# Low parts of 48 mix weight tiles per layer: a negating ScalarE copy and an accumulating DMA in place of subtractions

## The chip, the cores and the metric

The kernel runs on one core of a Trainium2 chip. The metric is the device time of one execution in microseconds (us), as the median of several runs. One execution was also taken by the hardware profiler. Engines are named as the profile names them: PE (TensorE matmul), PEld (its weight load), DVE (VectorE), ACT (ScalarE), POOL (GpSimd) and SP (SyncE, which only issues DMAs here).

## What is computed

A decoder trunk of two layers over 512 tokens of width 1024. Each layer has a token mixer with three gated branches, then a convolutional feed-forward part, each followed by a LayerNorm on a residual sum:

```python
h = layer_norm(x, ln_in_g, ln_in_b)
for l in range(DEPTH):                       # 2
    z = h @ w_in + b_in                      # pooling, conformer, q/k/v, indexer, three gates
    y_pool = pool_mixer(u_pool) @ w_pool_out
    y_conv = conformer_conv(u_conv) @ w_conv_out   # 31 taps, LayerNorm, swish
    y_attn = dsa_attention(...) @ w_attn_out       # indexer keeps the top 128 keys of a query
    merged = g0 * y_pool + g1 * y_conv + g2 * y_attn
    h = layer_norm(ALPHA * h + merged @ w_o)
    u = causal_dwconv(h @ w_up)
    h = layer_norm(ALPHA * h + (silu(gate) * val) @ w_down)
```

All of it is float32. A product of two float32 matrices is made of three passes: each operand is split into a high part (its value rounded to the matmul type `float32r`) and a low part (value minus high part), and high x high, high x low and low x high are summed.

## The kernel before, in words

**Weight tiles.** The weights of a layer are packed into 123 tiles of 128 x 1024 float32 (512 KB), in the order of use. `Weights.emit` (L66) prepares one: SP loads `w_raw` from memory (L70, two buffers), ACT copies it to the high part `w_hi` (L74, which rounds), and one engine subtracts, `w_lo = w_raw - w_hi` (L78). That engine is DVE (one instruction of 1024 columns), or POOL for the tiles listed in `W.side` (two instructions of 512 columns). In the mixer these are the nine tiles of `MIX_SIDE`; some more are listed around the end of each output projection. `w_hi` and `w_lo` have four buffers each. `Weights.take` (L83) hands out the next tile and first prepares all up to two tiles ahead.

**The mixer's tiles of a layer.** Tiles 0 to 2 are used beside the LayerNorm before. 3 to 16 are the other projections (indexer, pooling, conformer, v, q). 17 to 30 belong to branch A: a small tile that four steps share, four gate tiles, a second such five, four gates of branch C. 31 to 44 are the same for branch B. 45 to 48 are the attention output, 49 to 56 the output projection `w_o` in two halves of four. An ordinary projection tile makes 24 matmuls of 512 columns (`proj`, L282); its product lies in a PSUM bank of the kind "a", of which there are three, until ACT or DVE has read it.

**Work beside the tiles.** Generators are pumped between tiles (`step`, L398): on DVE the indexer (weighted sum of heads into `mask`, L475 and L477, then 16 rounds of MAX8 and MATCH_REPLACE, L484 and L485, for each of three query blocks), on ACT and POOL the conformer taps (ACT scales a shifted copy into `cvt`, L589; POOL adds it to `cv`, L590), then the softmax attention. In branch A DVE multiplies gate and branch product into `part` (L729), which frees a bank.

**The end of the mixer.** For each of eight column blocks `jt` DVE multiplies the last gate with the attention product (L762), POOL adds it to `part` (L763), ACT makes the high part of half the sum (L765) and DVE the low part (L766). After `jt == 3` the residual's LayerNorm scale and shift is issued: 16 POOL instructions (`residual`, L215, L220 and L221). Tiles 49 to 52, the first half of the output projection, each multiply two of the eight merged blocks (L316 to L318).

**Order.** Every engine executes its own instructions in order and waits in front of the first whose inputs or buffers aren't ready. The order is set before the run by a scheduler that places instructions by priority; the weight preparation runs at high priority (L73), so it moves up as far as its buffers let it.

Of the kernel before, what the change touches and what calls it, by code (L numbers as in the profile page):

```python
# [11 lines left out]
AF = mybir.ActivationFunctionType  # L12
ALU = mybir.AluOpType
# [30 lines left out]
N_CHUNK = 123  # L44
NSPLIT = {"mix": 3, "ffn": 3}
LAG = 2
MIX_SIDE = range(24, 42, 2)
ISSUE_ORDER = mybir.DependencyInfo(mybir.DependencyClass.NoSync, mybir.DependencyReason.DATA)
SIDE = 4
LN_POOL = ()  # L50
# [4 lines left out]
class Weights:  # L55
    def __init__(self, tc, w, raw_pool, split_pool, look, nchunk):
        self.tc, self.nc, self.w = tc, tc.nc, w
        self.raw_pool, self.split_pool = raw_pool, split_pool
        self.look = look
        self.n = nchunk  # L60
        self.emitted = 0
        self.used = 0
        self.ready = []
        self.side = set()

    def emit(self, upto):  # L66
        nc = self.nc
        while self.emitted < min(upto, self.n):
            raw = self.raw_pool.tile([P, D], F32, name="w_raw", tag="w_raw")
            nc.sync.dma_start(out=raw, in_=self.w[self.emitted])  # L70
            hi = self.split_pool.tile([P, D], F32R, name="w_hi", tag="w_hi")
            lo = self.split_pool.tile([P, D], F32R, name="w_lo", tag="w_lo")
            with self.tc.high_priority():  # L73
                nc.scalar.activation(hi, raw, AF.Copy)  # L74
                eng = nc.gpsimd if self.emitted in self.side else nc.vector
                for c in range(2 if self.emitted in self.side else 1):
                    cs = slice(512 * c, 512 * c + 512) if self.emitted in self.side else slice(0, D)
                    eng.tensor_tensor(out=lo[:, cs], in0=raw[:, cs], in1=hi[:, cs].bitcast(F32),  # L78
                                      op=ALU.subtract)
            self.ready.append((hi, lo))  # L80
            self.emitted += 1

    def take(self, look=None):  # L83
        self.emit(self.used + 1 + (self.look if look is None else look))
        self.used += 1
        return self.ready.pop(0)

# [2 lines left out]
def trunk_kernel(ctx, tc, x, positions, w, poolw, params, lnv, cons, out):  # L90
    nc = tc.nc
# [9 lines left out]
    W = Weights(tc, w, raw_pool, split_pool, 2, DEPTH * N_CHUNK)  # L101
# [253 lines left out]
    def mix(l, head, prev, ln, nxt):  # L355
        es = ExitStack()
        with es:
# [5 lines left out]
            def q_slot(tag, dt=F32R):  # L363
                return slot(tag, {"qa": 6, "qb": 4, "qc": 4}[tag], dt)
# [7 lines left out]
            def p_slot(dt=F32):  # L372
                return slot("part", 9, dt, [P, 528])
# [8 lines left out]
                return half_par[:, l, ct:ct + 1]  # L382

            bga, bgb = [], []
            W.side.update(l * N_CHUNK + i for i in MIX_SIDE)

            def pump(q, n):
                while q and n > 0:
# [366 lines left out]
            for jt in range(KT):  # L755
# [8 lines left out]
                hi, lo = q_slot("qa" if jt < 6 else "qb"), p_slot(F32R)[:, 0:L]  # L764
# [47 lines left out]
    for l in range(DEPTH):  # L812
        ffn_head = new_head("ffn")
        norm = mix(l, mix_head, norm, (1 + 2 * l, False), ffn_head)
        last = l == DEPTH - 1
        mix_head = None if last else new_head("mix")
        norm = ffn(l, ffn_head, norm, (2 + 2 * l, last), mix_head)
# [99 lines left out]
```

## Time and profile before

| | us |
|---|---|
| median of 3 runs | 1548.92 (1548.11 to 1550.29) |
| the profiled execution, its own time | 1548.56 |
| its span in the profile | 1546.8 |
| PE busy | 1467.5 (95%) |
| DVE busy | 1007.5 (65%) |
| ACT busy | 683.6 (44%) |
| POOL busy | 538.1 (35%) |

The span runs from the first to the last instruction. A busy share is a mean over stages that are limited by different things, so a share says little by itself. Matmuls overlap: one of 512 columns lasts 0.39 us, but the next starts before it ends, so PE can be shown busy all the time and still execute at different rates; the count of matmuls in a stretch tells more.

### The profile page before, as it was taken

The page shows a single profiled execution, that of the slowest core. Times are in us where ns is not written, and L with a number is a line of the kernel's source. Part 1 is how long each engine was busy: PE and PEld are TensorE (multiplying, and loading weights), DVE is VectorE, ACT ScalarE, POOL GpSimd, SP SyncE. Part 2 cuts the span into 40 slices and gives each one's busy share as a digit, 9 for nine tenths or more (in the row PEclk, how much of TensorE's full clock was granted, in tenths as well). Part 3 has the DMA queues.
Part 4 walks back from the last instruction along what each step waited for, and adds up shares of the span by engine and source line. Part 5 has one row for each costly group of instructions (what it writes and reads, how often), then busy time and mean ns, then how long its engine had stood idle before and what let it go on. Part 6 is the DMA issues. An engine that isn't in the chain of part 4 may idle for free.

```text
span 1546.8 us, 18617 instructions
## 1 busy us (share of the span) xinstructions
PE 1467.5 (95%) x6850; PEld 1218.1 (79%) x6850; DVE 1007.5 (65%) x1600; ACT 683.6 (44%) x1064; POOL 538.1 (35%) x395
## 2 busy tenths in 40 slices
PE   5998789999999999999999978999999999999997
PEld 5876678887888888888898756888878788888886
DVE  6799998756665555523268999976556655554234
ACT  5666636542444444421256664555326444443110
POOL 2357842209471111100134687231375511111004
PEclk9999999999999999999999989999999999999999
DMA  4422222223233333333234222222333333332331
GB/s 147 143 85 83 68 82 69 69 86 105 72 123 106 96 95 96 98 98 101 86 106 122 74 63 82 83 69 72 105 94 105 119 106 96 96 96 87 105 100 64
DMA packets 45019, 145.02 MB, mean 94 GB/s; under 512 B 6144, under 2 KB 7808, under 8 KB 44928
## 3 DMA queue, kind: packets, MB, share of 16 engines
q1 hardware_dynamic: 37632, 133.55, 28.1%
q10 hardware_dynamic: 7296, 10.29, 2.3%
q8 instruction: 54, 0.88, 0.2%
q14 instruction: 37, 0.30, 0.1%
HBM read 137.00 MB, written 2.10 MB: 90 GB/s over the span
## 4 chain that ended last, share of the span: by engine, by line
PE 70%; DVE 15%; POOL 7%; issue 4%; ACT 2%; DMA 2%; ACTq 0%; POOLq 0%; DVEq 0%
PE pb_a L289 15%; PE pb_a L290 15%; PE pb_a L291 15%; POOL h L221 3%; DVE w_lo L78 2%; POOL h L220 2%; PE pb_a L318 2%; PE pb_a L317 2%; PE pb_a L316 2%; DVE mask L477 2%; DVE mask L485 2%; PE pb_p L318 2%; PE pb_p L317 2%; PE pb_p L316 2%; PE pb_s L318 1%
## 5 line engine op out<-in xcount | busy, mean ns | idle before, releaser
L289 PE MATMUL pb_a<-hT_hi,w_hi 128*128 128x512 f32 (+1 forms) x1264 | 498.4, 394 | 35.8 <-DVE part L729 26.6
L78 DVE TENSOR_TENSOR w_lo<-w_raw,w_hi 128x1024 fp32r<-128x1024 f32 x210 | 290.3, 1383 | 339.9 <-ACT w_hi L74 338.9
L290 PE MATMUL pb_a<-hT_lo,w_hi 128*128 128x512 f32 (+1 forms) x1264 | 496.9, 393 | 0.0
L291 PE MATMUL pb_a<-hT_hi,w_lo 128*128 128x512 f32 (+1 forms) x1264 | 496.3, 393 | 0.0
L74 ACT ACTIVATE w_hi<-w_raw 128x1024 fp32r<-128x1024 f32 x246 | 260.6, 1059 | 400.0 <-PE pb_a L290 166.3
L289 PEld LDWEIGHTS pb_a<-hT_hi,w_hi 128*128 128x128 f32 x1264 | 241.2, 191 | 87.6 <-DVE part L729 29.9
L291 PEld LDWEIGHTS pb_a<-hT_hi,w_lo 128*128 128x128 f32 x1264 | 241.1, 191 | 47.4
L290 PEld LDWEIGHTS pb_a<-hT_lo,w_hi 128*128 128x128 f32 x1264 | 241.0, 191 | 46.5
L78 POOL TENSOR_TENSOR w_lo<-w_raw,w_hi 128x512 fp32r<-128x512 f32 x72 | 103.7, 1462 | 269.9 <-ACT w_hi L74 269.9
L800 POOL TENSOR_TENSOR fu<-fu 128x512 f32<-128x512 f32 x44 | 61.2, 1391 | 356.5 <-DVE fu L794 356.5
L590 POOL TENSOR_TENSOR cv<-cv,cvt 128x512 f32<-128x512 f32 x92 | 143.1, 1557 | 54.1 <-ACT cvt L589 46.5
L589 ACT ACTIVATE cvt<-cv,par 128x512 f32<-128x512 f32 x92 | 65.5, 721 | 28.0 <-POOL cv L590 27.7
L799 ACT ACTIVATE fu<-fu 128x512 f32<-128x512 f32 x44 | 27.8, 632 | 81.7 <-DVE fu L794 81.7
L794 DVE SCALAR_TENSOR_TENSOR fu<-pb_a,par,fu 128x510 f32<-128x510 f32 x82 | 61.4, 749 | 2.7
L791 ACT ACTIVATE fu<-pb_a,par 128x512 f32<-128x512 f32 x82 | 62.4, 761 | 0.0
L792 DVE SCALAR_TENSOR_TENSOR fu<-pb_a,par,fu 128x511 f32<-128x511 f32 x82 | 60.9, 743 | 0.0
L220 POOL TENSOR_TENSOR h<-h,gbt 128x512 f32<-128x512 f32 x32 | 52.1, 1660 | 18.3 <-DMA gbt<-in_lnv_dram 18.3
L683 ACT ACTIVATE qa<-qa,mx 128x128 f32<-128x128 f32 (+3 forms) x64 | 35.8, 560 | 51.1 <-DVE mx L680 48.2
L484 DVE MAX8 m<-mask 128x8 f32<-128x256 f32 (+2 forms) x96 | 52.8, 553 | 1.0
L208 ACT ACTIVATE gbt<-pb_a,par 128x128 f32<-128x128 f32 x96 | 35.7, 467 | 39.9 <-PE pb_a L200 39.9
L485 DVE MATCH_REPLACE8 mask<-m,mask 128x256 f32<-128x256 f32 (+2 forms) x96 | 51.9, 541 | 0.1
L316 PE MATMUL pb_a<-w_hi,g_hi 128*128 128x512 f32 x132 | 51.3, 389 | 0.0
(289 smaller groups left out, 2539.5 us busy)
## 6 DMA issues: line engine op xcount, KB each, us to landing
w_raw<-in_w_dram SPq DMA_DIRECT2D x246, 512.0 KB, 3.6
gbt<-in_lnv_dram ACTq DMA_DIRECT2D x20, 256.0 KB, 3.5
h<-in_x_dram SPq DMA_DIRECT2D x4, 512.0 KB, 5.5
t<-t ACTq DMA_DIRECT2D x32, 64.0 KB, 2.0
out_dram<-h SPq DMA_DIRECT2D x8, 256.0 KB, 2.0
part<-t ACTq DMA_DIRECT2D x32, 48.0 KB, 3.1
part<-t ACTq DMA_DIRECT2D x16, 64.0 KB, 4.1
par<-in_params_dram SPq DMA_DIRECT2D x2, 143.5 KB, 6.5
```

Source lines behind the costliest of these rows:

```text
L74: nc.scalar.activation(hi, raw, AF.Copy)
L78: eng.tensor_tensor(out=lo[:, cs], in0=raw[:, cs], in1=hi[:, cs].bitcast(F32), op=ALU.subtract)
L220: G.tensor_tensor(out=hb, in0=hb, in1=gb[0][c], op=ALU.mult)
L289: T.matmul(o, wh, xh(xc), start=(i == 0), stop=False)
L290: T.matmul(o, wh, xl(xc), start=False, stop=False)
L291: T.matmul(o, wl, xh(xc), start=False, stop=(i == n - 1))
L316: first = T.matmul(po[b], lh(k, b), wh, start=(k == 0), stop=False)
L318: T.matmul(po[b], ll(k, b), wh, start=False, stop=(k == nk - 1))
L485: V.match_replace(out=sc, in_to_replace=m8, in_values=sc, imm_value=FILL)
L589: A.activation(tm, hp[c][:, i:i + L], AF.Copy, scale=tap(i))
L590: G.tensor_tensor(out=pacc, in0=pacc, in1=tm, op=ALU.add)
L791: A.activation(t, o, AF.Identity, bias=par[:, l, PO_FB + ct:PO_FB + ct + 1], scale=tapw(2))
```

## The change

For tiles 7 to 54 of each layer (48 of 123), the low part is made in another way. ACT copies the raw tile into `w_lo` with scale -1, which gives minus the high part. POOL issues a DMA that reads the weight tile from memory once more and adds it to what lies in `w_lo`. ACT makes `w_hi` as before. DVE and POOL execute no subtraction for these tiles, and the list `MIX_SIDE` is gone; the other tiles are as before. When the tile that is taken is one of the 48, `take` prepares up to three tiles ahead, not two.

```diff
-MIX_SIDE = range(24, 42, 2)
+MIX_DMA = range(7, 55)
...
+            if self.emitted in self.by_dma:
+                with self.tc.high_priority():
+                    nc.scalar.activation(lo, raw, AF.Copy, scale=-1.0)
+                    nc.gpsimd.dma_start(out=lo, in_=self.w[self.emitted], accum_op=ALU.add)
+                    nc.scalar.activation(hi, raw, AF.Copy)
+                self.ready.append((hi, lo))
+                self.emitted += 1
+                continue
...
     def take(self, look=None):
-        self.emit(self.used + 1 + (self.look if look is None else look))
+        look = self.look + (self.used in self.by_dma) if look is None else look
+        self.emit(self.used + 1 + look)
...
-            W.side.update(l * N_CHUNK + i for i in MIX_SIDE)
+            W.by_dma.update(l * N_CHUNK + i for i in MIX_DMA)
```

The scheduler orders the whole program anew. Line numbers after the change are 10 higher behind `take`. Three places are shown.

ACT in branch A, first layer, before: a high part, then the gate's tanh out of the bank (`t<-pb_a`, L715), then indexer and tap work.

```order
L74 ACTIVATE w_hi_1584<-w_raw_1582 128x1024
L715 ACTIVATE t_1545<-pb_a_1520,half_par_89 128x512
L472 ACTIVATE u_1632<-pb_s_1629 128x512
L589 ACTIVATE cvt_1421<-cv_1021,par_74 128x512
L589 ACTIVATE cvt_1425<-cv_1021,par_74 128x512
```

The same gate after the change:

```order
L78 ACTIVATE w_hi_1537<-w_raw_1535 128x1024
L76 ACTIVATE w_lo_1538<-w_raw_1535 128x1024
L725 ACTIVATE t_1567<-pb_a_1542,half_par_89 128x512
L482 ACTIVATE u_1661<-pb_s_1658 128x512
L599 ACTIVATE cvt_1371<-cv_986,par_74 128x512
```

The negated copy stands between the high part and the reading of the bank. In both versions the tile that is prepared here is the third after the one whose product is read.

POOL in branch A, first layer, before, around the second of the tiles that it subtracts there, between conformer taps (`cv`):

```order
L590 TENSOR_TENSOR cv_1361<-cv_1361,cvt_1579 128x512
L78 TENSOR_TENSOR w_lo_1881<-w_raw_1878,w_hi_1880 128x512 x2
L590 TENSOR_TENSOR cv_1361<-cv_1361,cvt_1647 128x512
L590 TENSOR_TENSOR cv_1361<-cv_1361,cvt_1650 128x512
L590 TENSOR_TENSOR cv_1361<-cv_1361,cvt_1654 128x512
L590 TENSOR_TENSOR cv_1361<-cv_1361,cvt_1657 128x512
```

After the change, in the run of the same taps:

```order
L77 DMA w_lo_1906<-in_w_dram 128x1024
L600 TENSOR_TENSOR cv_1379<-cv_1379,cvt_1597 128x512
L600 TENSOR_TENSOR cv_1379<-cv_1379,cvt_1601 128x512
L600 TENSOR_TENSOR cv_1379<-cv_1379,cvt_1670 128x512
L600 TENSOR_TENSOR cv_1379<-cv_1379,cvt_1673 128x512
L77 DMA w_lo_1958<-in_w_dram 128x1024
```

Each tile now puts one DMA issue among two to four taps, where every second tile from 24 to 40 put two subtractions.

POOL at the end of the mixer, first layer, before: the last five of the eight sums `part`, with the residual's L220 and L221 between them.

```order
L763 TENSOR_TENSOR part_1703<-part_1703,t_3369 128x512
L221 TENSOR_TENSOR h_73<-h_73,gbt_3382 128x512 x4
L763 TENSOR_TENSOR part_1838<-part_1838,t_3423 128x512
L221 TENSOR_TENSOR h_73<-h_73,gbt_3385 128x512 x2
L763 TENSOR_TENSOR part_1919<-part_1919,t_3443 128x512
L221 TENSOR_TENSOR h_73<-h_73,gbt_3385 128x512 x2
L763 TENSOR_TENSOR part_1970<-part_1970,t_3469 128x512
L763 TENSOR_TENSOR part_2022<-part_2022,t_3489 128x512
```

After the change (`w_lo_3447`, `3494`, `3545`, `3576` and `3607` are tiles 50 to 54):

```order
L77 DMA w_lo_3447<-in_w_dram 128x1024
L231 TENSOR_TENSOR h_73<-h_73,gbt_3422 128x512
L773 TENSOR_TENSOR part_1863<-part_1863,t_3464 128x512
L231 TENSOR_TENSOR h_73<-h_73,gbt_3425 128x512
L773 TENSOR_TENSOR part_1944<-part_1944,t_3484 128x512
L231 TENSOR_TENSOR h_73<-h_73,gbt_3425 128x512
L77 DMA w_lo_3494<-in_w_dram 128x1024
L231 TENSOR_TENSOR h_73<-h_73,gbt_3425 128x512
L773 TENSOR_TENSOR part_1996<-part_1996,t_3511 128x512
L231 TENSOR_TENSOR h_73<-h_73,gbt_3425 128x512
L77 DMA w_lo_3545<-in_w_dram 128x1024
L773 TENSOR_TENSOR part_2048<-part_2048,t_3531 128x512
```

The issues for tiles 49 to 52 now stand in front of the eighth sum (that for tile 49 some rows above), three of them and one L231 less than before in front of the seventh. Those for 53 and 54 follow behind the eighth.

## Rows read from the trace of the kernel before

**Rows 1.** The page: busy us, share of the span and instructions, by engine.

```profile
PE 1467.5 (95%) x6850; PEld 1218.1 (79%) x6850; DVE 1007.5 (65%) x1600; ACT 683.6 (44%) x1064; POOL 538.1 (35%) x395
```

**Rows 2.** Stretches: busy us (instructions) by engine, granted clock, DMA share, GB/s.

```profile
80.00:240.00 160.00, 139.82 (x599) 112.50 (x599) 157.41 (x286) 89.83 (x145) 99.71 (x67) 0.94 0.26 80
840.00:1000.00 160.00, 138.76 (x595) 111.84 (x593) 157.47 (x289) 89.22 (x143) 100.42 (x66) 0.94 0.26 80
240.00:280.00 40.00, 40.00 (x201) 33.26 (x201) 31.66 (x84) 22.49 (x51) 12.19 (x10) 1.00 0.25 72
40.00:80.00 40.00, 38.12 (x197) 34.24 (x196) 32.63 (x36) 25.33 (x38) 16.24 (x14) 0.96 0.48 139
500.00:600.00 100.00, 100.00 (x443) 82.81 (x442) 52.86 (x63) 42.50 (x56) 12.57 (x10) 1.00 0.32 98
```

**Rows 3.** Waits of PE, 80 to 240 us: us in total, times, longest.

```profile
PE pb_a L289 <- DVE part L729: 13.3, 5, 5.7
PE pb_a L289 <- ACT t L662: 3.8, 1, 3.8
```

**Rows 4.** The chain of waits, 350 to 390 us: start, us, what.

```profile
355.18 2.27 POOL h L220
...
382.62 2.25 POOL part L763
...
384.88 0.64 ACT qb L765
...
385.55 1.09 DVE part L766
...
386.69 0.50 PE pb_a L318
```

**Rows 5.** The page's costliest groups: busy us, mean ns, idle before.

```profile
L78 DVE TENSOR_TENSOR w_lo<-w_raw,w_hi 128x1024 fp32r<-128x1024 f32 x210 | 290.3, 1383 | 339.9 <-ACT w_hi L74 338.9
L74 ACT ACTIVATE w_hi<-w_raw 128x1024 fp32r<-128x1024 f32 x246 | 260.6, 1059 | 400.0 <-PE pb_a L290 166.3
L78 POOL TENSOR_TENSOR w_lo<-w_raw,w_hi 128x512 fp32r<-128x512 f32 x72 | 103.7, 1462 | 269.9 <-ACT w_hi L74 269.9
```

**Rows 6.** Groups on DVE, first 80 to 240 us, then 840 to 1000 us.

```profile
L78 DVE TENSOR_TENSOR w_lo<-w_raw,w_hi 128x1024 fp32r<-128x1024 f32 x16 | 25.5, 1591 | 0.3 <-ACT w_hi L74 0.3
...
L78 DVE TENSOR_TENSOR w_lo<-w_raw,w_hi 128x1024 fp32r<-128x1024 f32 x16 | 25.2, 1576 | 0.3 <-ACT w_hi L74 0.3
```

**Rows 7.** Groups on ACT, 80 to 240 us.

```profile
L74 ACT ACTIVATE w_hi<-w_raw 128x1024 fp32r<-128x1024 f32 x22 | 23.2, 1054 | 17.1 <-PE pb_a L290 8.7 <-DMA w_raw<-in_w_dram 8.4
```

**Rows 8.** SP's issues of line L70: duration ns min/median/max.

```profile
L70 SPq DMA_DIRECT2D w_raw<-in_w_dram x246: 327/328/738, 4.9 to 1506.3; - x123
```

**Rows 9.** Groups on POOL, 80 to 240 us.

```profile
L590 POOL TENSOR_TENSOR cv<-cv,cvt 128x512 f32<-128x512 f32 x46 | 71.4, 1553 | 26.9 <-ACT cvt L589 24.4
L78 POOL TENSOR_TENSOR w_lo<-w_raw,w_hi 128x512 fp32r<-128x512 f32 x11 | 17.9, 1649 | 11.9 <-ACT w_hi L74 11.9
```

**Rows 10.** DMA queues (share of 16 engines) and issues (KB, median us to landing).

```profile
q1 hardware_dynamic: 37632, 133.55, 28.1%
...
w_raw<-in_w_dram SPq DMA_DIRECT2D x246, 512.0 KB, 3.6
...
t<-t ACTq DMA_DIRECT2D x32, 64.0 KB, 2.0
```

**Rows 11.** Timeline of PE around the last first-half matmuls of the output projection.

```profile
385.90 0.39 PE L317 MATMUL pb_a<-w_lo,qb 128*128 128x512 f32 x1
...
391.43 0.39 PE L318 MATMUL pb_v<-w_hi,part 128*128 128x512 f32 x1
```

**Rows 12.** Stretches with the fullest POOL, columns as in rows 2.

```profile
120.00:160.00 40.00, 32.81 (x131) 25.62 (x129) 39.49 (x59) 26.85 (x41) 31.19 (x19) 0.91 0.25 73
160.00:200.00 40.00, 32.48 (x133) 26.00 (x133) 39.66 (x60) 22.60 (x34) 36.58 (x24) 0.91 0.22 66
```

More of the change, by code (lines that the diff above doesn't have):

```diff
@@ L64, in __init__ @@
         self.side = set()
+        self.by_dma = set()
     def emit(self, upto):
```

## The prediction

> **What bounds the kernel now.** The page's first part shows PE busy for 95% of the span [rows 1], so I ask where the other time is. The busy times by stretch say it [rows 2]. From 240 to 280 us, and in the feed-forward part (500 to 600 us), PE is busy throughout at a granted clock of 1.00; 443 matmuls in 100 us is one in 0.2257 us. From 80 to 240 us, in the first layer's mixer, and from 840 to 1000 us, in the second's, it is not: PE is busy for 139.8 and 138.8 of 160 us, at a mean clock of 0.94, so a part of the stretch is spent at the lower of its two levels, 1.2 GHz. DVE is busy for 157.4 of 160 us there. The list of waits agrees: PE waits longest for DVE's product `part`, which frees a PSUM bank [rows 3]. Here DVE is the bound. PE's work of that stretch would take 139.8 x 0.94 = 131 us at full clock.
>
> The second place is the end of the mixer. The chain of waits runs over POOL alone from 355.2 us until the seventh of the eight sums `part` at 384.9 us, then over one ACT and one DVE instruction to PE [rows 4]. Whatever is put on POOL in front of that sum arrives at PE undiminished.
>
> **What the change removes.** 96 tiles lose their subtraction. Of these 18 (nine per layer) were POOL's and 78 DVE's, 78 x 1.38 = 108 us of DVE and 36 x 1.46 = 53 us of POOL [rows 5]. Only what lies in the DVE-bound stretch counts: 16 subtractions, 25.5 us in one layer and 25.2 us in the other [rows 6], longer than the mean since POOL works beside them. Without them DVE has 157.4 - 25.5 = 132 us, PE 131 us. So 28 us per layer is the most that the stretch can give. Both engines can't be full at once: from 40 to 80 us PE reached 38.1 of 40 us beside a DVE with 32.6 [rows 2]. I let the stretch end at 142 us, with both at 93%: a gain of 18 us per layer, bounds 12 and 24. Outside the stretch PE already is full, so a freer DVE or POOL gives nothing.
>
> **What it adds on ACT.** 96 negated copies; the nearest row is the copy of the same tile, 1.06 us [rows 5], in sum 102 us. ACT was busy for 89.8 of the 160 us [rows 2]; 22 tiles are prepared there [rows 7], so it rises to 113 of 142 us, 80%. I cost this at nothing, covered by ACT's idle time. If that cover is gone, the tanh behind the copy reads its PSUM bank 1.06 us later; there are three such banks.
>
> **What it adds on POOL: the issue.** The trace has no DMA issued by POOL. From below, SP issues the same 128 x 1024 tile in 0.33 us [rows 8]; from above, POOL walks such a tile itself in two subtractions, 2 x 1.46 = 2.9 us [rows 5]. I take 1.0 us, nearer to the lower end, since an issue touches no data. In the stretch POOL then has 99.7 - 17.4 (its 11 subtractions by the stretch's busy time, for which the group says 17.9 [rows 9]) + 22 x 1.0 = 104 us: no bound.
>
> **What it adds on the DMA engines.** 96 transfers of 512 KB. The raw load of such a tile lands 3.6 us after its issue, and its queue moves 133.55 MB in 28.1% of the span, so a tile takes 512 KB / 307 GB/s = 1.7 us of the engines [rows 10]. The accumulating one must in addition read what it adds to: I take 3.6 + 1.7 = 5.3 us from issue to landing, an estimate. Bounds: 3.6 us, and 16 us, which is eight times the 2.0 us of a 64 KB copy within SBUF [rows 10]. The engines' share of 26% in the stretch then rises to about 80% (0.26 x 160 / 142, and 22 x 3.4 / 142 for two reads each). The Trainium skill, "DMA: Bandwidth & Descriptors", section "Anatomy of one DMA — SWDGE (gpsimd) path", gives a DMA issued from GpSimd about 2.0 us plus its bytes at 436 GB/s; for 512 KB that would be an estimate of 3.2 us. No run here shows that yet. By it, the loss at the mixer's end below would be 3.8 us and the sum 1520 us, by the rows 1525 us.
>
> **Is the low part in time?** It now passes ACT twice (2.1 us), perhaps one tap on POOL (1.55 us [rows 9]) and the DMA (5.3 us): 9 us. While a small tile of a branch keeps one of the four buffers, tile n + 3 takes the buffer of tile n, so two tiles' time is there: 160 us / 22 tiles is 7.3 us a tile now, 142 / 22 = 6.5 us then, so 13 us. It is hidden, with 4 us left. The look three ahead costs nothing by itself; it uses the spare buffer that the longer path needs.
>
> **The mixer's end.** POOL issues for tiles 49, 50 and 51 ahead of the seventh sum, for 52 between the seventh and eighth. Before, the eighth sum followed the seventh without a gap; it ended 1.2 us later, at 386.1 us. Four issues put it at 386.1 + 4 = 390.1 us. Tile 52's issue starts 2.2 us before that and lands 5.3 us after its start, at 393.2 us. PE waits for it: all but 4 of the 24 matmuls of that tile stand behind its first low part, 20 x 0.2257 = 4.5 us, so the half ends at 397.7 us. Before, its last matmul started at 391.43 and lasted 0.39 us [rows 11]. Loss: 6 us per layer, in general three issues plus the landing minus 2.4 us. The two tiles after that, 53 and 54, land within these 4.5 us or soon after it. No DVE time that is saved here helps, since POOL sets this end.
>
> **Sum.** Against the profiled execution's own 1548.6 us: -2 x 18 + 2 x 6 = -24, so **1525 us**. (The median of the runs shown is 0.4 us above that execution.) The forecast's own range is -2 x 24 + 2 x 4 = 1509 to -2 x 12 + 2 x 10 = 1545 us. A change of 0.2%, 3.1 us, is about what a measurement of this kernel can tell from none.
>
> **Rivals.**
> - *A slow POOL issue (slower).* POOL stands between ACT and the DMA in one queue with the conformer taps and the residual. Against it: POOL is idle for 60 of the 160 us. For it: its highest share in 80 us is (31.19 + 36.58) / 80 = 85% [rows 12], because the taps wait for ACT. With an issue of d us the stretch can't be shorter than (82.3 + 22 d) / 0.85, and the end costs 4 d + 1.9. From d = 2.05 the two cancel. At 2.5 us the stretch is 161.5 us and the end loses 11.9: 1548.6 + 2 x 13.4 = 1575 us. The Trainium skill, same page, section "SWDGE vs HWDGE vs iDMA", speaks for it: an accumulating DMA can only be issued from GpSimd, whose cores compute the descriptors in software.
> - *A slow transfer (slower).* If the add takes the DMA engines far longer than a read, the path is no longer hidden: over about 9.4 us landing the buffers' turn sets the pace. At 16 us three buffers turn in 2.1 + 1.55 + 16 + 5.4 (24 matmuls) = 25 us, 8.4 us a tile: 9 us lost on branch A's eight gates against 7.3, 13 on branch B's (30 matmuls there, 6.8 us), 11 still won on the 14 tiles before, and 16.6 lost at the end: 28 us per layer, 1604 us. From about 12 us landing on it is no gain. For it: an accumulation is nowhere in the trace; against: plain copies run at 307 GB/s.
> - *The wait only moves (no change).* PE's second wait there is for ACT (`t`, L662) [rows 3], and ACT gets every negated copy ahead of a bank. With 7 us of gain and 6 of loss per layer: 1547 us.
> - *The end is covered (faster still).* Two stretches at DVE's and PE's floor, with nearly nothing lost at the end: -2 x 25, 1499 us. It needs a landing near 3.6 us and an issue near 0.33 us.
>
> **Chances.** Forecast 0.57: the bound engine loses 25 us in a stretch with nothing else full, which is the firmest row here. Covered end 0.07; wait moved 0.10 (0.06 within 0.2%, 0.02 on each side); slow issue 0.13; slow transfer 0.13. Faster: 0.57 + 0.07 + 0.02 = 0.66; the same: 0.06; slower: 0.02 + 0.13 + 0.13 = 0.28. The range goes from 1505 to 1578 us: it leaves out most of the covered end (0.05), the upper half of the slow issue (0.06) and most of the slow transfer (0.09).
>
> **What would show it.** Right: DVE at about 132 us in stretches of about 142, PE's wait for `part` nearly gone, no PE wait for `w_lo` in the branches, POOL's issue near 1 us, landings near 5 us, PE waiting some us for `w_lo` in the last first-half tile of the output projection. Wrong: PE waiting for the accumulating DMA in branch A or B (slow transfer), a POOL that is full from 80 us on (slow issue), PE's idle time put down to ACT (wait moved).

## The result: slower by 0.7%, where a gain was forecast

| | before | after |
|---|---|---|
| median of 4 runs, us | 1548.95 | 1559.1 (1555.76 to 1562.33) |
| ratio, 95% interval | | 1.0066 [1.0052, 1.008] |
| the profiled execution, us | 1548.56 | 1556.89 |

The forecast was 1525 us, a gain; the kernel became slower. The page of the profile after the change, first the engines, then the queue and the issues of the new DMA, the row of the negated copy and the landing (columns as in [rows 1, 5, 10]):

```profile
PE 1467.9 (94%) x6850; PEld 1222.2 (79%) x6850; DVE 913.8 (59%) x1522; ACT 769.7 (49%) x1160; POOL 531.1 (34%) x455
...
q0 software_dynamic: 13824, 50.34, 18.2%
...
L77 POOL DMA_DIRECT2D w_lo<-in_w_dram x96 | 85.9, 895 | 231.9 <-ACT w_lo L76 228.4
...
L76 ACT ACTIVATE w_lo<-w_raw 128x1024 fp32r<-128x1024 f32 x96 | 100.5, 1047 | 38.3 <-PE pb_a L327 29.1
...
w_lo<-in_w_dram POOLq DMA_DIRECT2D x96, 512.0 KB, 7.6
```

DVE did lose its work (1007.5 to 913.8 us), and the issue is short: 0.895 us. A landing takes 7.6 us; 50.34 MB in 18.2% of 1555.1 us is 2.95 us of the engines for a tile, against 1.7 for a plain load [rows 10]. The row to note is L77's idle time: over both layers POOL stood for 228 us in front of its issues until ACT's negated copy was there.

Busy times by stretch, after (the first two answer to [rows 2]):

```profile
core 0: us, PE busy (x) PEld busy (x) DVE busy (x) ACT busy (x) POOL busy (x), PEclk, DMA share, GB/s
80.00:240.00 160.00, 146.22 (x641) 118.44 (x641) 141.56 (x287) 115.08 (x178) 99.43 (x82) 0.96 0.74 164
840.00:1000.00 160.00, 149.44 (x648) 121.85 (x647) 140.76 (x288) 117.83 (x183) 99.69 (x83) 0.95 0.76 166
320.00:360.00 40.00, 36.49 (x159) 29.07 (x157) 15.77 (x19) 16.85 (x22) 18.11 (x16) 0.96 0.66 155
360.00:400.00 40.00, 31.32 (x125) 24.96 (x124) 19.64 (x18) 11.23 (x14) 21.76 (x19) 0.87 0.58 121
```

DVE is no longer full in the two mixer stretches and PE makes 42 and 53 more matmuls in them. PE falls back at the mixer's end: 125 matmuls in the last 40 us at a mean clock of 0.87, where before it made 159 in these 40 us at 1.00.

Where the time went is read from the timeline, from the start of the same instruction in both programs (lines after the change are 10 higher). The last column is the run "tiles 17 to 44" below.

| start of, us | before | after | tiles 17 to 44 |
|---|---|---|---|
| first tanh of branch A (L715) | 146.9 | 151.8 | 147.9 |
| fourth late gate (L735) | 239.1 | 229.2 | 230.6 |
| eighth late gate | 342.6 | 333.0 | 333.8 |
| first attention product (L762) | 345.2 | 340.8 | 336.4 |
| first sum into h (L323) | 389.8 | 394.1 | 381.0 |
| second layer: eighth late gate | 1100.4 | 1092.4 | 1078.9 |
| second layer: first attention product | 1103.0 | 1100.1 | 1081.5 |
| second layer: first sum into h | 1147.6 | 1152.9 | 1126.1 |

In the first layer 4.9 us are lost by the start of branch A, 14.8 won up to the fourth late gate, 0.3 lost to the eighth, 5.2 lost before the first attention product and 8.7 from there to h: +4.3 us. The second layer adds about 1 us more. That is 5.3 us, and 4.8 at the last normalization (L184, at 1541.3 and 1546.1 us). The profiled executions differ by 8.3 us; the rest lies behind the last work, from that normalization to the end of the span: 5.5 us before, 9.1 after. POOL's closing DRAIN (before, then after; the longest of three) lasts 6.86 us in place of 1.15, until 1554.3 us, where SP has ended its own at 1550.8.

```profile
L913 POOLq DRAIN  x3: 34/78/1152, 1542.7 to 1546.5; - x3
...
L923 POOLq DRAIN  x3: 40/102/6855, 1547.5 to 1554.8; - x3
```

It is longer in every kernel below that issues DMAs on POOL, from 3.46 us with 28 issues to 6.86 with 96; the one that issues none has 1.16 us. It comes once in an execution. What it waits for isn't shown.

Most of the 8.7 us stand in one row of DVE (L776 makes the low part of a merged block, L772 the product of gate and attention). The timeline after the change (start, duration, engine, instruction; in brackets the idle time before it and its releaser), DVE first:

```profile
349.54 0.15 DVE L162 COPY gbt<-hT_lo 128x1 f32<-128x1 f32 x1
351.14 0.69 DVE L776 SCALAR_TENSOR_TENSOR part<-part,qa 128x512 fp32r<-128x512 f32 x1 [1.45 <-ACT qa L775]
351.75 0.68 DVE L772 SCALAR_TENSOR_TENSOR t<-cv,pb_a 128x512 f32<-128x512 f32 x1
353.99 14.29 DVE L776 SCALAR_TENSOR_TENSOR part<-part,qa 128x512 fp32r<-128x512 f32 x1 [1.56 <-ACT qa L775]
368.20 1.87 DVE L772 SCALAR_TENSOR_TENSOR t<-cv,pb_a 128x512 f32<-128x512 f32 x3
```

and POOL:

```profile
351.14 0.83 POOL L77 DMA_DIRECT2D w_lo<-in_w_dram  x1
351.75 1.54 POOL L773 TENSOR_TENSOR part<-part,t 128x512 f32<-128x512 f32 x1
353.00 5.26 POOL L230 TENSOR_TENSOR h<-h,gbt 128x512 f32<-128x512 f32 x4
358.00 2.73 POOL L231 TENSOR_TENSOR h<-h,gbt 128x512 f32<-128x512 f32 x2
360.48 1.46 POOL L773 TENSOR_TENSOR part<-part,t 128x512 f32<-128x512 f32 x1
361.70 1.46 POOL L231 TENSOR_TENSOR h<-h,gbt 128x512 f32<-128x512 f32 x1
362.91 1.09 POOL L77 DMA_DIRECT2D w_lo<-in_w_dram  x1
363.52 1.77 POOL L231 TENSOR_TENSOR h<-h,gbt 128x512 f32<-128x512 f32 x1
364.74 1.76 POOL L773 TENSOR_TENSOR part<-part,t 128x512 f32<-128x512 f32 x1
365.96 1.76 POOL L231 TENSOR_TENSOR h<-h,gbt 128x512 f32<-128x512 f32 x1
368.96 1.28 POOL L773 TENSOR_TENSOR part<-part,t 128x512 f32<-128x512 f32 x1 [1.24 <-DVE t L772]
```

An instruction whose median is 0.69 us takes 14.29. It ends as POOL comes to its first pause (367.7 to 368.96 us), and POOL pauses only because its next sum needs the product L772 that stands behind the stuck DVE instruction. L772 also frees PE's bank. The list of PE's waits from 80 to 400 us, first layer, after (in total, times, longest):

```profile
PE pb_a L326 <- DVE t L772: 8.7, 1, 8.7
PE pb_s L479 <- ACT u L482: 5.4, 2, 4.9
PE pb_a L299 <- ACT qa_hi L714: 3.5, 1, 3.5
...
PE pb_a L301 <- DMA w_lo<-in_w_dram: 2.2, 3, 1.0
...
PE pb_a L299 <- DVE part L739: 0.9, 1, 0.9
```

The wait for branch A's product [rows 3] is nearly gone, as forecast; the largest is now the one behind the stuck instruction. The second layer has its twin, of 14.30 us. In the kernel before, POOL works there without a long pause as well [rows 4], but the same DVE instruction takes at most 1.8 us (shortest, median and longest in ns, both layers):

```profile
L766 DVE SCALAR_TENSOR_TENSOR part<-part,qa x12: 684/1101/1776, 348.4 to 1138.2; 128x512 fp32r<-128x512 f32 x12
```

### The profile page after: what moved, and what is told of

Same layout as the page of the kernel before. It is cut to its first block, busy times and chain, and to the rows that moved or that the text cites. A ratio compares the mean times of both kernels' runs of the same rounds, so it can differ in the third digit from the quotient of the medians.

```text
span 1555.1 us, 18747 instructions
## 1 busy us (share of the span) xinstructions
PE 1467.9 (94%) x6850; PEld 1222.2 (79%) x6850; DVE 913.8 (59%) x1522; ACT 769.7 (49%) x1160; POOL 531.1 (34%) x455
## 3 DMA queue, kind: packets, MB, share of 16 engines
q0 software_dynamic: 13824, 50.34, 18.2%
## 4 chain that ended last, share of the span: by engine, by line
PE 69%; DVE 8%; DMA 6%; ACT 6%; POOL 6%; issue 5%; ACTq 0%; POOLq 0%; DVEq 0%
PE pb_a L299 14%; PE pb_a L300 14%; PE pb_a L301 14%; PE pb_a L326 3%; PE pb_a L328 3%; PE pb_a L327 3%; DMA part<-t 2%; PE pb_p L328 2%; PE pb_p L327 2%; PE pb_s L326 2%; PE pb_s L328 2%; PE pb_p L326 2%; PE pb_s L327 2%; DMA w_raw<-in_w_dram 1%; POOL h L230 1%
## 5 line engine op out<-in xcount | busy, mean ns | idle before, releaser
L87 DVE TENSOR_TENSOR w_lo<-w_raw,w_hi 128x1024 fp32r<-128x1024 f32 x132 | 171.0, 1296 | 327.7 <-ACT w_hi L83 322.4
L77 POOL DMA_DIRECT2D w_lo<-in_w_dram x96 | 85.9, 895 | 231.9 <-ACT w_lo L76 228.4
L600 POOL TENSOR_TENSOR cv<-cv,cvt 128x512 f32<-128x512 f32 x92 | 134.6, 1464 | 14.5 <-ACT cvt L599 10.5
L87 POOL TENSOR_TENSOR w_lo<-w_raw,w_hi 128x512 fp32r<-128x512 f32 x36 | 49.7, 1401 | 224.9 <-ACT w_hi L83 224.9
L76 ACT ACTIVATE w_lo<-w_raw 128x1024 fp32r<-128x1024 f32 x96 | 100.5, 1047 | 38.3 <-PE pb_a L327 29.1
L230 POOL TENSOR_TENSOR h<-h,gbt 128x512 f32<-128x512 f32 x32 | 47.7, 1571 | 18.3 <-DMA gbt<-in_lnv_dram 16.4
```

What stands on the lines that cost most here:

```text
L76: nc.scalar.activation(lo, raw, AF.Copy, scale=-1.0)
L77: nc.gpsimd.dma_start(out=lo, in_=self.w[self.emitted], accum_op=ALU.add)
L600: G.tensor_tensor(out=pacc, in0=pacc, in1=tm, op=ALU.add)
```

## Experiments

Times are medians; the intervals are of the ratio to the kernel before on the same chip. Diffs are against the changed kernel where nothing else is said.

**1. Which tiles.** Three runs move the two ends of the list.

```diff
-MIX_DMA = range(7, 55)
+MIX_DMA = range(7, 45)
```

> Tiles 45 to 54 (attention output, first six of the output projection) are subtracted by DVE again; tiles 7 to 44 keep the accumulating DMA. Theory: the loss of 9.6 + 4.3 = 14 us per layer between the eighth late gate and the last h comes from the DMAs issued and the copies queued in that stretch. Then 28 us come back: 1559 - 28 = 1531 us, and the low part L776 has no instruction over 3 us. Rival: POOL's sums and residual set that end whatever the tiles do, and time won in branch A is only waited away there: 1547 to 1559 us.

Measured 1538.4 us, 0.9935 [0.9922, 0.9948]: 21 of the 28 us came back. L776, its instructions and their shortest, median and longest time in ns:

```profile
L776 DVE SCALAR_TENSOR_TENSOR part<-part,qa x12: 684/1104/1773, 343.0 to 1124.8; 128x512 fp32r<-128x512 f32 x12
```

From the first attention product to h it is 339.8 to 384.4 = 44.6 us, exactly as before the change (345.2 to 389.8). The wait ahead of that product stayed.

```diff
-MIX_DMA = range(7, 55)
+MIX_DMA = range(17, 45)
```

> Only tiles 17 to 44 (branches A and B) keep the accumulating DMA. Theory: beside the end (14 us per layer) the mixer's start loses 5 us per layer to tiles 7 to 16 (POOL waits 4 to 5 us at the issue for ACT's negated copy with the pooling sums behind it). Both undone: 1559 - 2 x 19 = 1521 us. Rival: the start's 5 us come from the freer branch A starting later, not from tiles 7 to 16: like the run with tiles 7 to 44.

Measured 1530.6 us, 0.9879 [0.9865, 0.9893], 28.5 of 38 us back, between the two expectations: the fastest of the kernels that compute the whole. By the table above its gain is made in branch A, 8.5 us by the fourth late gate, and kept. The 5.2 us ahead of the attention product are gone with tiles 7 to 16, so in the change those were their doing too. Attention doesn't start late (its first L690 at 214.9 us, against 216.8 here) but ends late: its last high part (L714) is made at 335.0 us, behind the eighth late gate, against 332.2 here, ahead of it.

```diff
-MIX_DMA = range(7, 55)
+MIX_DMA = range(17, 55)
```

> Tiles 17 to 54 keep the accumulating DMA, 7 to 16 are subtracted by DVE. Theory: 5 us per layer back at the start, the end unchanged: 1559 - 10 = 1549 us. Rival: the end takes up what the start gives: 1557 to 1560 us.

1554.7 us, 1.0041 [1.0029, 1.0053], between the two. Against the run 17 to 44, the end's ten tiles cost 24 us here (12 a layer); a long L776 is there.

```diff
-MIX_DMA = range(7, 55)
+MIX_DMA = range(17, 31)
```

> Only tiles 17 to 30 (branch A) keep the accumulating DMA. Theory: the whole gain of the run with 17 to 44 is branch A's, where DVE is full, and branch B, where PE is full, gives and takes nothing: 1528 to 1533 us. Rival: the freer DVE in branch B is worth something, or its DMAs cost something: outside of that.

1534.4 us, 0.99 [0.9885, 0.9915]: just outside, 3.8 us above the run 17 to 44. In the second layer the first attention product comes 9.1 us after the eighth late gate (1089.7 against 1080.6), in the run 17 to 44 2.6 us. So DVE's time in branch B, where PE is full, is worth something: attention's softmax is made there, and what isn't done in time PE waits for at the end.

**2. What stops DVE at the end.**

```diff
-        def residual(self):
+        def residual(self, eng=G):
...
-                    G.tensor_tensor(out=hb, in0=hb, in1=gb[0][c], op=ALU.mult)
-                    G.tensor_tensor(out=hb, in0=hb, in1=gb[1][c], op=ALU.add)
+                    eng.tensor_tensor(out=hb, in0=hb, in1=gb[0][c], op=ALU.mult)
+                    eng.tensor_tensor(out=hb, in0=hb, in1=gb[1][c], op=ALU.add)
...
-                    prev.residual()
+                    prev.residual(V)
```

> All 48 tiles as in the change, but the residual's 16 products and sums at the mixer's end run on DVE in place of POOL. Theory of the port: the low part L776 that takes 14.3 us stands still because DVE and POOL share a way into SBUF and POOL runs without a pause from 353.0 to 367.7 us. Then no L776 takes over 3 us, and PE's waits of 9 us for DVE's t go: 1559 - 2 x 9 = 1541 us. Rival (queues): ACT's negated copies wait for a buffer and the high parts of the merged blocks wait behind them, which the residual has no part in: 1556 to 1562 us, and a long L776 stays.

1545.7 us, 0.9984 [0.9965, 1.0003]; 13 us came back, of 18 expected. Its twelve executions spread from 1540.3 to 1556.8 us; the rows are of one that took 1541.95, and no trace shows what made two of them take 1556.4 and 1556.8:

```profile
L776 DVE SCALAR_TENSOR_TENSOR part<-part,qa x12: 676/685/1473, 346.4 to 1118.8; 128x512 fp32r<-128x512 f32 x12
```

DVE got 16 instructions more per layer and the stall went from both layers. Every negated copy and every issue is still there, so the rival falls (though the scheduler moved a few of ACT's instructions too): without the residual on POOL this execution has no stall. Why did DVE get its turn before the change? The next runs take the DMA at the end apart (tiles 17 to 44 keep it).

```diff
-MIX_DMA = range(7, 55)
+MIX_DMA = range(17, 55)
...
-                    nc.gpsimd.dma_start(out=lo, in_=self.w[self.emitted], accum_op=ALU.add)
+                    if self.emitted % N_CHUNK in range(17, 45):
+                        nc.gpsimd.dma_start(out=lo, in_=self.w[self.emitted], accum_op=ALU.add)
```

> Tiles 17 to 54 as in the run with 17 to 54, but for tiles 45 to 54 POOL issues no DMA: ACT's negated copy alone is left in w_lo (the low part of these ten tiles is left out). The trace shows POOL starting each instruction 0.24 to 0.55 us before the one ahead has ended once it has issued a DMA, and 0.04 us before it otherwise. Theory: this overlap is why DVE's low part L776 finds no gap between POOL's. Without the issues no L776 takes over 3 us, and the time comes near to that of the run with 17 to 44: 1531 to 1540 us. Rival: it is ACT's copies, which hold up the merged high parts, or the missing subtractions on DVE: a long L776 stays, 1550 to 1556 us.

1523.7 us, 0.9846 [0.9829, 0.9863], 31 us under the run with the DMAs: ACT's copies and the missing subtractions on DVE are not what costs. (These ten tiles have no low part here; DVE subtracts them in neither run.) But in the profiled execution (1529.8 us, the other three took 1522.9 to 1524.2) one layer had a long instruction without any issue:

```profile
L777 DVE SCALAR_TENSOR_TENSOR part<-part,qa x12: 683/898/10996, 336.8 to 1114.9; 128x512 fp32r<-128x512 f32 x12
```

So the kernel was run once more:

> The run without DMA issues for tiles 45 to 54 once more (the low part of these ten tiles is left out). Theory: without an issue the long low part is an exception: none of over 3 us in either layer, and 1522 to 1526 us. Rival: it comes without an issue as well: again one of over 10 us, and 1528 to 1532 us.

```profile
L777 DVE SCALAR_TENSOR_TENSOR part<-part,qa x12: 685/1104/1859, 336.8 to 1110.5; 128x512 fp32r<-128x512 f32 x12
```

1525.6 us, a single run: none. So without issues one of the four layers traced has it; with them both layers of each kernel that has accumulating DMAs there and the residual on POOL. Next, the bytes:

```diff
-MIX_DMA = range(7, 55)
+MIX_DMA = range(17, 55)
...
-                    nc.gpsimd.dma_start(out=lo, in_=self.w[self.emitted], accum_op=ALU.add)
+                    c = D if self.emitted % N_CHUNK in range(17, 45) else 16
+                    nc.gpsimd.dma_start(out=lo[:, 0:c], in_=self.w[self.emitted][:, 0:c], accum_op=ALU.add)
```

> Tiles 17 to 54 as in the run with 17 to 54, but for tiles 45 to 54 POOL's DMA adds only 16 of the 1024 columns (their low part is left out but for those columns). Theory of the issue: POOL runs one instruction ahead after it has issued, so DVE's low part finds no gap: L776 takes 14 us in both layers and the time is 1548 to 1555 us. Rival (the transfer, its landing of 7.6 us or its traffic into SBUF): no long L776, 1522 to 1532 us.

1553.5 us, 1.0031 [1.0019, 1.0042], with 14.29 and 14.28 us in the two layers:

```profile
348.09 14.29 DVE L777 SCALAR_TENSOR_TENSOR part<-part,qa 128x512 fp32r<-128x512 f32 x1 [1.52 <-ACT qa L776]
...
1107.25 14.28 DVE L777 SCALAR_TENSOR_TENSOR part<-part,qa 128x512 fp32r<-128x512 f32 x1 [1.64 <-ACT qa L776]
```

One 64th of the bytes, and 1.2 us of difference: transfer and landing have no part in the end's loss. Last, the issue by itself, added to the best kernel (diff against it):

```diff
+            if self.emitted % N_CHUNK in range(45, 55):
+                with self.tc.high_priority():
+                    scr = self.sm.tile([P, 8], F32, name="m8")
+                    nc.gpsimd.dma_start(out=scr, in_=hi[:, 0:8].bitcast(F32))
```

> As the run with tiles 17 to 44 (1531 us); for tiles 45 to 54 POOL issues in addition a DMA that copies 8 columns of the high part into a scratch tile that nobody reads. DVE subtracts as in that run, ACT makes no negated copy there, nothing waits for the DMA. Theory: the issue alone makes POOL run one instruction ahead, DVE's low part finds no gap, takes 10 us or more in both layers, and the time is 1545 to 1556 us. Rival: DVE's own subtractions between keep it in turn with POOL, or it takes the accumulating copies: no instruction of DVE over 3 us there, and only POOL's ten issues cost, 1531 to 1539 us.

1552.6 us, 1.0021 [1.0012, 1.003]: 22 us lost to twenty DMAs that nobody waits for. From the first attention product to h it is 54.4 us in both layers, 9.8 more than in the run 17 to 44. DVE's timeline:

```profile
351.77 8.47 DVE L781 SCALAR_TENSOR_TENSOR part<-part,qa 128x512 fp32r<-128x512 f32 x1 [1.39 <-ACT qa L780]
360.16 0.67 DVE L777 SCALAR_TENSOR_TENSOR t<-cv,pb_a 128x512 f32<-128x512 f32 x1
360.76 6.75 DVE L87 TENSOR_TENSOR w_lo<-w_raw,w_hi 128x1024 fp32r<-128x1024 f32 x1
```

and POOL's:

```profile
349.18 0.56 POOL L92 DMA_DIRECT2D m<-w_hi  x1
349.76 1.31 POOL L778 TENSOR_TENSOR part<-part,t 128x512 f32<-128x512 f32 x1
351.01 5.01 POOL L235 TENSOR_TENSOR h<-h,gbt 128x512 f32<-128x512 f32 x4
355.98 1.26 POOL L778 TENSOR_TENSOR part<-part,t 128x512 f32<-128x512 f32 x1
357.21 2.48 POOL L236 TENSOR_TENSOR h<-h,gbt 128x512 f32<-128x512 f32 x2
359.64 0.57 POOL L92 DMA_DIRECT2D m<-w_hi  x1
360.23 2.52 POOL L236 TENSOR_TENSOR h<-h,gbt 128x512 f32<-128x512 f32 x2
...
366.37 0.56 POOL L92 DMA_DIRECT2D m<-w_hi  x1
```

Both DVE instructions stand from soon after one issue until the next, the two layers alike (8.47 and 8.47 us, 6.75 and 6.76). DVE comes in only at POOL's next issue, where POOL works on no data. (In the changed kernel the issue at 362.91 us did not let it in.) So the issue is enough, and the rival falls, though the instruction is shorter than I wrote. The overlap that my expectations named as its way is not it: here a POOL instruction starts 0.04 to 0.06 us before the one ahead ends (351.01 against 351.07), as without issues, and DVE stands all the same.

How turns were taken otherwise is seen in the run 17 to 44, in the same place: four residual instructions in 6.48 us, where POOL alone needs 5.01, since DVE comes in between.

```profile
350.37 6.48 POOL L230 TENSOR_TENSOR h<-h,gbt 128x512 f32<-128x512 f32 x4
```

Two runs at the end told less. The residual in four parts:

```diff
-                if jt == 3:
-                    prev.residual()
+                if jt in range(3, 7):
+                    prev.residual([jt - 3])
```

> All 48 tiles as in the change; the residual's 16 POOL instructions are issued in four parts of four, behind the merged blocks 3, 4, 5 and 6, in place of all behind block 3. Theory of the port: POOL's run without a pause is cut to at most 4 residual instructions, 2 issues and 2 sums, some 10 us, so no L776 takes over 8 us; PE loses at most 3 us there instead of 9: 1545 to 1553 us. Rival: the length of POOL's run has no part in it: a long L776 of 14 us stays, 1556 to 1562 us.

1559.2 us, 1.007 [1.0058, 1.0083], and an L778 of 14.29 us. This doesn't count against POOL's run: the scheduler put POOL's instructions nearly where they were (four, two, one residual instruction between the sums, as above), so the edit made no cut. And ACT's order:

```diff
+                    nc.scalar.activation(hi, raw, AF.Copy)
                     nc.scalar.activation(lo, raw, AF.Copy, scale=-1.0)
                     nc.gpsimd.dma_start(out=lo, in_=self.w[self.emitted], accum_op=ALU.add)
-                    nc.scalar.activation(hi, raw, AF.Copy)
```

> All 48 tiles as in the change, only that ACT makes the high part first and the negated copy after it, so that each DMA is issued about 1 us later and each high part is there 1 us earlier. Theory: neither order touches POOL's run at the end: the long L776 stays, 1556 to 1564 us. Rival: the high part behind the negated copy is what PE waits for: under 1554 us.

1554.7 us, 1.004 [1.0027, 1.0052], between the two expectations. The long L776 stays (14.28 and 14.29 us). The interval touches the change's own, and the two profiled executions differ by 1.6 us only; by these, something is won before the end (the fourth late gate starts at 227.1 us, against 229.2).

**3. What is lost at the start.** Tiles 7 to 44, with no DMA for 7 to 16:

```diff
-MIX_DMA = range(7, 55)
+MIX_DMA = range(7, 45)
...
-                    nc.gpsimd.dma_start(out=lo, in_=self.w[self.emitted], accum_op=ALU.add)
+                    if self.emitted % N_CHUNK in range(17, 45):
+                        nc.gpsimd.dma_start(out=lo, in_=self.w[self.emitted], accum_op=ALU.add)
```

> Tiles 7 to 44 as in the run with 7 to 44, but for tiles 7 to 16 POOL issues no DMA (their low part is left out, w_lo keeps ACT's negated copy). Theory: the start is lost to the DMAs, by their share of the engines (0.80 from 40 to 80 us) and by POOL's waits at the issue with the pooling sums behind it: as the run with 17 to 44, 1529 to 1533 us. Rival: it is ACT's second copy per tile: as the run with 7 to 44, 1536 to 1541 us.

1519.4 us, 0.9818 [0.9803, 0.9834], below both expectations: 11 us under the run 17 to 44, 19 under the run 7 to 44. No cost of ACT's second copy shows; the DMAs at the start cost 19 us, where the subtractions they replace cost 11, net of the copies. Their bytes or their issues?

```diff
-MIX_DMA = range(7, 55)
+MIX_DMA = range(7, 45)
...
-                    nc.gpsimd.dma_start(out=lo, in_=self.w[self.emitted], accum_op=ALU.add)
+                    c = D if self.emitted % N_CHUNK in range(17, 45) else 16
+                    nc.gpsimd.dma_start(out=lo[:, 0:c], in_=self.w[self.emitted][:, 0:c], accum_op=ALU.add)
```

> Tiles 7 to 44 as in the run with 7 to 44, but for tiles 7 to 16 POOL's DMA adds only 16 of the 1024 columns (their low part is left out but for those columns). POOL's issue, and its wait for ACT's negated copy, stay; 63 of 64 of the bytes go. Theory of the transfer: the start's 19 us (1538 against 1519 without these DMAs) are the bytes, with the DMA engines at 0.8 to 0.95 from 40 to 100 us: 1519 to 1525 us. Rival (POOL's queue): the pooling sums and rotary products wait behind issues whose copy is not there yet: 1533 to 1539 us.

1533.7 us, 0.99 [0.9884, 0.9916]: 14 of the 19 us stay with nearly no bytes. My theory falls, the rival holds; the bytes are worth 5 us. It isn't the stall of the mixer's end: the longest DVE instruction takes 2.2 us from 40 to 150 us, and 3.4 us at the second layer's start. POOL's waits from 40 to 110 us in this run (in total, times, longest):

```profile
POOL w_lo L78 <- ACT w_lo L76: 17.1, 6, 6.1
```

What stands behind such a wait is seen in the timeline of this run:

```profile
81.98 0.86 POOL L78 DMA_DIRECT2D w_lo<-in_w_dram  x1 [4.79 <-ACT w_lo L76]
82.54 1.39 POOL L521 TENSOR_TENSOR part<-part 128x527 f32<-128x527 f32 x1
```

and without the DMAs:

```profile
74.64 1.06 POOL L521 TENSOR_TENSOR part<-part 128x527 f32<-128x527 f32 x1
```

The second pooling sum starts 7.9 us later, and attention's last high part is made 7.2 us later (332.3 against 325.1). It is the same in the change:

```profile
84.66 0.86 POOL L77 DMA_DIRECT2D w_lo<-in_w_dram  x1 [4.98 <-ACT w_lo L76]
85.22 1.39 POOL L520 TENSOR_TENSOR part<-part 128x527 f32<-128x527 f32 x1
```

and before:

```profile
75.19 1.16 POOL L510 TENSOR_TENSOR part<-part 128x527 f32<-128x527 f32 x1 [2.86 <-ACT u L472]
```

There it starts 10 us later. A last run puts another POOL instruction with the same kind of wait there, on top of the run 17 to 44:

```diff
-MIX_DMA = range(7, 55)
+MIX_DMA = range(17, 45)
...
             W.by_dma.update(l * N_CHUNK + i for i in MIX_DMA)
+            W.side.update(l * N_CHUNK + i for i in range(8, 17, 2))
```

> As the run with tiles 17 to 44, and tiles 8, 10, 12, 14 and 16 are subtracted by POOL (two instructions of 512 columns) in place of DVE. Theory: DVE is full from 80 us on (38.4 of 40), so five subtractions of 1.4 to 1.6 us less per layer are worth 3 to 7 us per layer where POOL is idle for half: 1517 to 1525 us. Rival: POOL's pooling sums come later, or DVE slows beside POOL, and nothing is won: 1529 to 1534 us.

1541.2 us, 0.9957 [0.9944, 0.9971], 11 us worse than without and above both expectations. Fewer subtractions for DVE, no DMA more, and again POOL stands in front of a weight tile:

```profile
POOL w_lo L87 <- ACT w_hi L83: 15.9, 4, 5.4
```

The second pooling sum starts at 80.6 us, against 75.2. So POOL's place in line is the likely price at the start, whether it issues or subtracts. The other half of the rival, a DVE that slows beside POOL, isn't told apart from it: six of DVE's taps (L606, or L605; 40 to 150 us) take 1.53 us each here, against 1.23 in the run 17 to 44, and 1.43 with thin DMAs against 1.23 without.

**4. The look-ahead.** The kernel before, with three tiles ahead:

```diff
-        self.emit(self.used + 1 + (self.look if look is None else look))
+        if look is None:
+            look = self.look + (self.used % N_CHUNK in range(7, 55))
+        self.emit(self.used + 1 + look)
```

> The kernel before, only that three tiles are prepared ahead for tiles 7 to 54, as the change does, and all subtractions stay. Theory: the earlier preparation by itself gives and takes nothing, since DVE is full in the branches: 1546 to 1552 us. Rival: part of the branches' gain, or of the end's loss, is the look-ahead's: under 1545, or over 1553 us.

1548.7 us, 1.0001 [0.9992, 1.001]: nothing, as expected.

## Why the prediction was wrong

- *"Here DVE is the bound", 80 to 240 us.* Right for branch A: without its subtractions the time from its first tanh to the fourth late gate is shorter in every run, 77.4 us after the change against 92.2 before.
- *"A gain of 18 us per layer, bounds 12 and 24."* Mis-sized: the lead at the eighth late gate is 9.6 us in the first layer. Of 14.8 won in branch A, 4.9 had just been lost at the start. What failed is that nothing was costed for tiles 7 to 16: POOL's busy time (99.4 of 160 us, where I had 104 of 142) gave "no bound", but POOL executes in order and stood in front of issues whose copy wasn't there. Without these DMAs, and without their low parts, the lead is 14.5 us (328.1 against 342.6).
- *ACT's copies cost nothing.* Nothing speaks against it: both runs that keep the copies and leave out DMAs are faster than the run 17 to 44. But they leave out DVE's subtractions as well, so a small cost could be hidden.
- *The issue, 1.0 us.* Right as a duration (0.895). As a cost it was not: at the end twenty issues of 0.56 us cost 22 us.
- *The landing, 5.3 us.* Mis-sized: 7.6 us, from 5.2 to 9.7. The Trainium skill's page "DMA: Bandwidth & Descriptors" (section "Anatomy of one DMA — SWDGE (gpsimd) path"), from which I had an estimate of 3.2 us, is further off; the trace doesn't agree. It hardly mattered: PE's waits for `w_lo` from 80 to 400 us are 2.2 us in all, so *the low part is in time* held.
- *"Loss: 6 us per layer" at the mixer's end.* This is the step that turned the sign: without the end's tiles the kernel gains (1538.4 us), without the start's it still loses (1554.7). The table has 5.2 + 8.7 = 13.9 us in the first layer, 5.1 + 8.2 = 13.3 in the second; the first terms, ahead of the attention product, are the start's doing, and the second, 8.7 and 8.2, stand against the 6. By the runs the end's tiles cost 10 to 12 us a layer against tiles that DVE subtracts. I had read rows 4 as a chain on POOL to which each issue adds its own time, "No DVE time that is saved here helps, since POOL sets this end". POOL's eighth sum did not come 4 us later but earlier: it started at 376.8 us, where seventh and eighth had started from 382.6 on [rows 4]. It was DVE that stood, and PE behind it; the forecast wait of PE for `w_lo` in the output projection (L327) doesn't come. In rows 4 one residual instruction takes 2.27 us, where POOL alone needs 1.25 (four in 5.01): a turn of DVE lies in it. I read that as POOL's own time.
- *"Outside the stretch PE already is full, so a freer DVE or POOL gives nothing."* Wrong by a little: branch B's tiles are worth 3.8 us.
- *The sum.* -18 + 6 = -12 us a layer became -9.6 + 13.9 = +4.3 in the first and -12.3 + 13.3 = +1.0 in the second (8.0 earlier at the eighth late gate, with 4.3 brought along); with the 3 us net that follow, 3.5 of them behind the last work with POOL's closing DRAIN, which had no term, that is 8.3, the difference of the two profiled executions.
- *The rivals.* A slow POOL issue came nearest, a loss through POOL's queue at start and end; but its condition, 2.05 us an issue, wasn't met. A slow transfer, the wait moved to ACT, and the covered end did not come. (For an issue of d us the forecast's own form of the end's loss, "three issues plus the landing minus 2.4", gives 3 d + 2.9, where this rival has 4 d + 1.9; they agree at 1 us only.)

## What to carry to other kernels

An instruction on an in-order engine costs what stands behind it while it waits for its input; the engine's busy share doesn't show that. Work moved to POOL belongs where POOL's queue is short of urgent work and has pauses in which DVE comes in: here in the branches (tiles 17 to 44, 1530.6 us, 1.2% better than the kernel before; POOL is busy for 99 of 160 us from 80 to 240 us, and in the branches no DVE instruction of any run takes 1.5 us more than the median of its kind), not at the mixer's start or end. Look for single instructions many times over their median; one such row was the largest part of this result.

## What the hardware showed that I had not expected

DVE's low part (two inputs from SBUF) stood still for as long as POOL worked on SBUF data without a pause: 14.3 us against 0.69. The Trainium skill, "SBUF — State Buffer", section "Who interferes with whom", says that such a DVE instruction contends with a GpSimd instruction that reads SBUF, that the shared port pair is an exclusive lock, and that the order of issue decides who blocks. The trace agrees that DVE stands, and with the run that moved the residual off POOL. But DVE's wait wasn't over with one instruction of POOL, of 1.25 us: in the changed kernel it lasted over eleven. Issues among POOL's instructions at the mixer's end make it so, whatever they move: in both layers of five kernels (14.2 to 14.3 us), and in both of the kernel with idle issues (8.47 us). Without issues there it came in one layer of four where DVE doesn't subtract, and in none of the kernels where it does (at most 1.8 us). What in the issue changes the turns stays open.
